# A hybrid attention and RWKV step on one core: the recurrence's products that share a moving operand are joined in pairs

## The chip, the cores and the metric

The kernel runs on one core of a Trainium2 chip (trn2). The metric is the device time of one execution in microseconds. The profile is one execution of the same program, taken by the hardware profiler.

## What is computed

One layer of a streaming encoder, in fp32, for a prompt of 2048 rows and a sample of 32 rows. The projection of the normalised input is split among eight stick-breaking attention heads and eight RWKV-7 heads; both results are joined, projected by `w_out`, and a SwiGLU layer follows. The change touches the RWKV heads, whose definition is a recurrence over the rows:

```python
def _rwkv7_scan(wkv0, r, log_w, k, v, kk, a):
    def step(S, inp):
        r_t, lw_t, k_t, v_t, kk_t, a_t = inp
        sa = jnp.einsum('bhvk,bhk->bhv', S, kk_t)
        S = (S * jnp.exp(lw_t)[:, :, None, :]
             - sa[..., :, None] * (kk_t * a_t)[..., None, :]
             + v_t[..., :, None] * k_t[..., None, :])
        return S, jnp.einsum('bhvk,bhk->bhv', S, r_t)
```

`S` is a state of 64 x 64 for each head. The rows' outputs are then normalised by head, scaled, and written into the mix that the output projection reads.

## The kernel before

The kernel has three stages, one after the other, whose instructions a planner in the build step places on each engine's queue by priority and by when it expects operands and buffers.

The first stage projects the input, and prepares, for each chunk of 64 rows (`CH`; 32 chunks of the prompt and one of the sample) and each head, what the recurrence needs: `QR_d` holds the decayed `kk` and `r` (64 columns each), `KBt_d` the decayed `k` and `kk * a`, `A4_d` their masked products with `QR` (mask `mA`), and `Tinv_d` the inverses of the diagonal blocks of one of them (`inverse`). All are written to DRAM.

The second stage is the one in question. Three generators run in it together: `attention`, `recurrence` and `first_rows` (the output projection of the first 1024 rows). A loop (lines 1170 to 1180) takes the generator that has advanced least, by the work it has yielded (a rough number of microseconds of TensorE) divided by a number of its own: 385 for attention, 230 for the recurrence, which starts at 25, and 155 for the rows, which start at 60. So the yields of the recurrence decide how much of the others' work lies between its steps.

The recurrence works through the chunks in order, the sample first. In each chunk, for eight heads, five groups of small fp32 products go one after the other through one PSUM buffer (`psR`): `up` (line 1095) takes the chunk's `kk` part of `QA` times `VST`, in whose lower partitions are the values and in whose upper ones the state; `sap` (1105) multiplies by the inverse `TTt`; `snp` (1114) multiplies `KBt` by `VS` and gives the new state, which DVE sums (1119) and scales by the decay (1121); `yp` (1127 and 1129) gives the output, `QA`'s `r` part times `VST` plus `AB` times `VS`, which ACT copies into `Yt` (1132). In between, `merge1` and `merge2` complete the inverse of the next chunk by two groups of products of 32 x 32. Each product is issued as two instructions, so a group of eight heads has 16. `fetch` loads the operands of the chunk after the next. After two chunks, `normalise` works on `Yt` on DVE, ACT and POOL in four steps, one at each `step_tail()`, and its columns are transposed and written to the mix.

Attention's products are on operands split into two rounded parts (`fp32r`); its scores become weights by a sigmoid on ACT (777) and a scan along the row on DVE (779), are transposed on TensorE (838), split again by ACT and DVE (105, 106) and multiplied by the values (852, 853).

The third stage finishes the output projection and computes the SwiGLU layer.

Of the kernel before, what the change touches and what calls it, by code (L numbers as in the profile page):

```python
# [24 lines left out]
H = 8  # L25
# [27 lines left out]
def kernel(ctx: ExitStack, tc: tile.TileContext, x_prompt, x_sample, cache_k, cache_v,  # L53
# [61 lines left out]
    with tc.tile_pool(name="pa0", bufs=1) as pe, tc.tile_pool(name="pa1", bufs=1) as pa, \  # L115
# [74 lines left out]
        for r in (0, 64):  # L190
            POOL.affine_select(mA[r:r + 64, 0:64], mA[r:r + 64, 0:64], [[1, 64]], ALU.is_gt, 0.0,
                               base=0, channel_multiplier=-1)
            POOL.affine_select(mA[r:r + 64, 64:128], mA[r:r + 64, 64:128], [[1, 64]], ALU.is_ge, 0.0,
                               base=0, channel_multiplier=-1)
# [69 lines left out]
        def superblock(sb, T0, NTILE):  # L264
# [154 lines left out]
            def g_k(w, c):  # L419
# [47 lines left out]
                def stage3(av, E65, Em, nrm):  # L467
# [6 lines left out]
                    POOL.tensor_tensor(QR[:, 0:NC, 0:64], c3(kk), E65[:, 0:NC, 0:64], ALU.mult)  # L474
                    POOL.tensor_tensor(QR[:, 0:NC, 64:128], c3(rr), E65[:, 0:NC, 1:65], ALU.mult)
# [52 lines left out]
            def inverse(c):  # L528
# [6 lines left out]
                for (jb, nj, d_) in blocks:  # L535
                    for h_ in range(4):
                        SP.dma_start(At[n + h_:n + 4 * nj:4], A4_d[jb:jb + nj, 64 + 32 * d_:96 + 32 * d_, hs + h_,
                                                                   32 * d_:32 * d_ + 32])
# [225 lines left out]
    with tc.tile_pool(reuse_waits="tile", name="bp", bufs=6) as bp, \  # L764
# [237 lines left out]
        def recurrence():  # L1002
# [11 lines left out]
            def fetch(ch):  # L1014
# [5 lines left out]
                KBt = br.tile([P, 512], F32, tag="KBt", name="KBtc")  # L1020
                SP.dma_start(KBt, KBt_d[ch])
                AB = br.tile([P, H, P], F32, tag="AB", name="ABc")
                SP.dma_start(AB[up_], A4_d[ch, 64:128])
# [18 lines left out]
                return [QA, KBt, AB, VS, VST, TTt, T1]  # L1042

            def merge1(c):
# [5 lines left out]
                for h in range(H):  # L1050
                    PE.matmul(mp[96:128, h * 32:(h + 1) * 32], AB[64:96, h, 32:64], T1[64:96, h, :],
# [37 lines left out]
            for ci, ch in enumerate(seq):  # L1089
                samp = ch == NCH  # L1090
                QA, KBt, AB, VS, VST, TTt, _ = cur
                heads = [(h, slice(h * 64, (h + 1) * 64)) for h in range(H)]
                up = psR.tile([P, 512], F32, tag="rw", name="up")
                for h, hs in heads:
                    PE.matmul(up[up_, hs], QA[:, h, 0:64], VST[:, hs], start=True, stop=True)
                Us = br.tile([P, 512], F32, tag="Us", name="Us")
                DVE.tensor_copy(Us[up_], up[up_])
                yield 0.85
# [14 lines left out]
                for h, hs in heads:  # L1113
                    PE.matmul(np_[up_, hs], KBt[:, hs], VS[:, hs], start=True, stop=True)
# [4 lines left out]
                DVE.tensor_tensor(Sn[up_], np_[up_], VST[up_], ALU.add)  # L1119
                s3 = Sn[up_].rearrange("p (h v) -> p h v", h=H)  # L1120
                DVE.tensor_tensor(s3, s3, PC[up_, ch, :].unsqueeze(2).to_broadcast([64, H, 64]), ALU.mult)
                yield 0.85
                step_tail()
                yp = psR.tile([P, 512], F32, tag="rw", name="yp")
                e = 0 if samp else 64 * (ch % 2)
                for h, hs in heads:
                    PE.matmul(yp[e:e + 64, hs], QA[:, h, 64:128], VST[:, hs], start=h == 0, stop=False)
# [344 lines left out]
```

## Time and profile before

| | us |
|---|---|
| median of three runs | 3404.04 |
| lowest and highest run | 3403.97, 3408.7 |
| the profiled execution | 3404.64 |
| its span, first to last instruction | 3402.5 |

In the profile, PE is TensorE's matrix multiplication and PEld its loading of weights, which overlaps it; DVE is VectorE, ACT is ScalarE, POOL is GpSimd and SP is SyncE, which issues DMAs here. A form such as 128*64 128x64 says: 128 rows and 64 columns of weights, and a moving operand of 128 partitions with 64 columns. A row of the timeline merges instructions of one line that follow each other; its duration reaches to the end of the last one, which for PE lies beyond the start of the next row, since products are pipelined. An entry in square brackets is idle time before it and what ended it.

### The profile page before, as it was taken

To read this page: it belongs to the slowest core of one execution; us is meant where nothing else is said; L and a number is where in the kernel's file an instruction comes from. 1 tells how busy PE (TensorE), PEld (TensorE's weight loads), DVE (VectorE), ACT (ScalarE), POOL (GpSimd) and SP (SyncE) were. 2 spreads that over 40 slices of the span, in tenths; PEclk is the share of its full clock that TensorE was granted. 3 is DMA by queue.
4 is the path that set the end of the run, shared out by engine and by line. 5 is a ranking of instruction groups with operands and counts; after the bars stand their busy time and mean duration, and the time that the engine had idled before them with its cause. 6 is when DMAs were issued, how large, how long until landed. Compare 5 with 4: busy or idle time off the path is not lost. (4 is left out here: it accounts for less than half of the span.)

```text
span 3402.5 us, 54147 instructions
## 1 busy us (share of the span) xinstructions
PE 3183.6 (94%) x20661; PEld 2835.4 (83%) x20661; DVE 2233.9 (66%) x3283; ACT 1407.5 (41%) x2768; POOL 1330.4 (39%) x1119
## 2 busy tenths in 40 slices
PE   7998998989779999999998899999899999999998
PEld 7987898878667777877886788899788999899998
DVE  4675757678768887887772566555755555665555
ACT  6434344444245564555542433333422333433333
POOL 3423423244201121112223555555544554466654
PEclk9999999989889999999999999999999999999999
DMA  5555564565675656565544533222633222432221
GB/s 149 157 163 144 165 192 138 154 185 157 198 206 142 165 150 164 150 161 160 156 118 150 183 113 108 83 75 75 206 100 90 84 66 71 144 101 81 81 87 63
DMA packets 542955, 453.74 MB, mean 133 GB/s; under 512 B 74580, under 2 KB 450976, under 8 KB 542696
## 3 DMA queue, kind: packets, MB, share of 16 engines
q1 hardware_dynamic: 454168, 404.26, 41.0%
q10 hardware_dynamic: 88528, 46.02, 5.0%
q8 instruction: 164, 2.69, 0.3%
q14 instruction: 95, 0.78, 0.1%
HBM read 325.64 MB, written 124.53 MB: 132 GB/s over the span
## 5 line engine op out<-in xcount | busy, mean ns | idle before, releaser
L106 POOL TENSOR_TENSOR al<-s,ah 128x512 fp32r<-128x512 f32 x198 | 258.0, 1303 | 558.5 <-ACT ah L105 557.7
L1405 DVE TENSOR_TENSOR x<-x,dn 128x512 f32<-128x512 f32 x374 | 255.1, 686 | 222.8 <-PE dn L1402 222.6
L779 DVE TENSOR_TENSOR_SCAN R<-R,z 128x512 f32<-128x512 f32 (+2 forms) x320 | 338.5, 1084 | 77.2 <-ACT R L777 74.7
L1402 PE MATMUL dn<-dh,hdh 128*128 128x512 f32 x748 | 296.2, 397 | 19.2 <-ACT hdh L105 18.9
L1402 PE MATMUL dn<-dh,hdl 128*128 128x512 f32 x748 | 297.5, 398 | 5.7 <-DVE hdl L106 5.5
L1402 PE MATMUL dn<-dl,hdh 128*128 128x512 f32 x748 | 296.1, 396 | 0.0
L325 PE MATMUL mm<-hh,wh 128*128 128x384 f32 (+4 forms) x1296 | 248.7, 333 | 2.5 <-ACT xp L337 1.5
L105 ACT CAST dh<-rawd 128x1024 fp32r<-128x1024 f32 x66 | 66.2, 1049 | 430.2 <-PE dn L1402 430.2
L105 ACT CAST ah<-s 128x512 fp32r<-128x512 f32 x264 | 163.4, 621 | 183.3 <-PE pt L1356 68.0
L325 PE MATMUL mm<-hh,wl 128*128 128x384 f32 (+4 forms) x1296 | 234.0, 323 | 0.0
L325 PE MATMUL mm<-hl,wh 128*128 128x384 f32 (+4 forms) x1296 | 233.2, 322 | 0.0
L777 ACT ACTIVATE R<-z 128x512 f32<-128x512 f32 (+2 forms) x320 | 163.4, 535 | 159.1 <-PE z L826 98.5
L325 PEld LDWEIGHTS mm<-hh,wh 128*128 128x128 f32 (+1 forms) x1296 | 211.2, 192 | 9.9 <-ACT xp L337 2.2
L325 PEld LDWEIGHTS mm<-hh,wl 128*128 128x128 f32 (+1 forms) x1296 | 210.2, 189 | 2.6
L325 PEld LDWEIGHTS mm<-hl,wh 128*128 128x128 f32 (+1 forms) x1296 | 209.3, 188 | 2.6
L106 DVE TENSOR_TENSOR wtl<-wt,wth 128x512 fp32r<-128x512 f32 (+1 forms) x320 | 179.0, 596 | 15.5 <-ACT wth L105 14.2
L1402 PEld LDWEIGHTS dn<-dh,hdh 128*128 128x128 f32 x748 | 139.2, 186 | 54.6 <-ACT hdh L105 22.3
L105 ACT CAST wth<-wt 128x512 fp32r<-128x512 f32 (+1 forms) x320 | 156.3, 529 | 53.9 <-PE wt L838 51.7
L1402 PEld LDWEIGHTS dn<-dh,hdl 128*128 128x128 f32 x748 | 139.5, 186 | 40.8 <-DVE hdl L106 8.9
L838 PE MATMUL wt<-ident,R 128*128 128x128 f32 x1088 | 164.6, 281 | 9.4 <-DVE wtl L106 8.6
L1029 POOL MEMSET TTt<- 32x512 f32 x33 | 17.2, 521 | 392.5 <-PE sap L1105 272.3
L1402 PEld LDWEIGHTS dn<-dl,hdh 128*128 128x128 f32 x748 | 139.6, 187 | 33.5
(397 smaller groups left out, 7900.6 us busy)
## 6 DMA issues: line engine op xcount, KB each, us to landing
wraw<-in_w_in ACTq DMA_DIRECT2D x77, 512.0 KB
rawu<-in_w_up SPq DMA_DIRECT2D x66, 512.0 KB
rawg<-in_w_gate SPq DMA_DIRECT2D x66, 512.0 KB
rawd<-in_w_down SPq DMA_DIRECT2D x66, 512.0 KB
A_d<-a SPq DMA_DIRECT2D x28, 512.0 KB
mx<-mixT_d SPq DMA_DIRECT2D x27, 512.0 KB
k<-khl_d SPq DMA_DIRECT2D x42, 256.0 KB
vp<-vhl_d SPq DMA_DIRECT2D x42, 256.0 KB
```

The lines of the kernel that those rows point to most:

```text
L105: ACT.copy(hi, src)
L106: (eng or DVE).tensor_tensor(lo, src, f32(hi), ALU.subtract)
L325: PE.matmul(ps[0:wd, 0:s1 - s0], a_[:, kt, 0:wd], b_[:, kt, s0:s1], start=i == 0, stop=i == 3 * KT - 1)
L777: ACT.activation(R[:, 0:n], z[:, 0:n], AF.Sigmoid, scale=-0.125)
L779: DVE.tensor_tensor_scan(rv, rv, z[:, 0:n], before, ALU.mult, ALU.bypass)
L838: PE.transpose(pt[:, j * P:(j + 1) * P], state[h, qg, kc, j][:, kb * P:(kb + 1) * P], ident)
L1029: POOL.memset(TTt[96:128], 0.0)
L1402: PE.matmul(ps[0:n], a_[:, i * P:i * P + n], b_[:, ds_], start=k == 0, stop=k == 3 * len(js) - 1)
L1405: DVE.tensor_tensor(x1[:n, ds_], x1[:n, ds_], ps[0:n], ALU.add)
```

## The change

`up` and `yp`'s first group have the same moving operand, `VST`, and both take half of `QA` as weights: they become one group with 128 output rows, 0 to 63 the first share of the output and 64 to 127 the old `up`. `snp` and `yp`'s second group have the same moving operand `VS` and become one too, with weights `KA`: columns 64 to 127 hold `KBt`, columns 0 to 63 hold `AB`'s output part in the upper partitions and zeros in the lower ones. The two shares of the output can no longer add up in PSUM, since each is in another group: the first is copied with `Us` by DVE, the second by ACT into `y2`, and GpSimd adds them into `Yt`. The halves of `QR` and of the mask change places, so that the rows land on the right partitions. `AB` shrinks to the 32 rows and columns that `merge1` reads, in one buffer. The `yp` step vanishes, and the yields around it with the divisor of the generator (182 for 230) are set anew.

```diff
--- before.py
+++ after.py
@@ -188,9 +188,9 @@
         mA = pe.tile([P, P], F32, name="mA")
         POOL.memset(mA, 1.0)
         for r in (0, 64):
-            POOL.affine_select(mA[r:r + 64, 0:64], mA[r:r + 64, 0:64], [[1, 64]], ALU.is_gt, 0.0,
+            POOL.affine_select(mA[r:r + 64, 64:128], mA[r:r + 64, 64:128], [[1, 64]], ALU.is_gt, 0.0,
                                base=0, channel_multiplier=-1)
-            POOL.affine_select(mA[r:r + 64, 64:128], mA[r:r + 64, 64:128], [[1, 64]], ALU.is_ge, 0.0,
+            POOL.affine_select(mA[r:r + 64, 0:64], mA[r:r + 64, 0:64], [[1, 64]], ALU.is_ge, 0.0,
                                base=0, channel_multiplier=-1)
         DVE.memset(m64, 1.0)
         DVE.memset(m64.rearrange("p (c t) -> p c t", t=CH)[:, :, 0:1], 0.0)
@@ -471,8 +471,8 @@
                                              ALU.mult, ALU.mult)
                     KB = pe.tile([P, 12, P], F32, tag="KB", name="KB")
                     QR = pe.tile([P, 12, P], F32, tag="QR", name="QR")
-                    POOL.tensor_tensor(QR[:, 0:NC, 0:64], c3(kk), E65[:, 0:NC, 0:64], ALU.mult)
-                    POOL.tensor_tensor(QR[:, 0:NC, 64:128], c3(rr), E65[:, 0:NC, 1:65], ALU.mult)
+                    POOL.tensor_tensor(QR[:, 0:NC, 64:128], c3(kk), E65[:, 0:NC, 0:64], ALU.mult)
+                    POOL.tensor_tensor(QR[:, 0:NC, 0:64], c3(rr), E65[:, 0:NC, 1:65], ALU.mult)
                     POOL.tensor_tensor(kk[:, 0:WT], kk[:, 0:WT], av[:, 0:WT], ALU.mult)
                     POOL.tensor_tensor(KB[:, 0:NC, 64:128], c3(kk), c3(Em), ALU.mult)
                     DVE.tensor_scalar(av[:, 0:WT], av[:, 0:WT], -1.0, col(R_KA + c), ALU.add, ALU.mult)
@@ -535,7 +535,7 @@
                 for (jb, nj, d_) in blocks:
                     for h_ in range(4):
                         SP.dma_start(At[n + h_:n + 4 * nj:4], A4_d[jb:jb + nj, 64 + 32 * d_:96 + 32 * d_, hs + h_,
-                                                                   32 * d_:32 * d_ + 32])
+                                                                   64 + 32 * d_:96 + 32 * d_])
                     n += 4 * nj
                 POOL.memset(Ti[0:n], 0.0)
                 POOL.memset(Ti[0:n].rearrange("p a b -> p (a b)")[:, 0:1024:33], 1.0)
@@ -1017,10 +1017,15 @@
                 QA = br.tile([P, H, P], F32, tag="QA", name="QAc")
                 SP.dma_start(QA[up_], QR_d[ch].rearrange("c (e n) t -> n (c e) t", n=64))
                 SP.dma_start(QA[0:64], A4_d[ch, 0:64])
-                KBt = br.tile([P, 512], F32, tag="KBt", name="KBtc")
-                SP.dma_start(KBt, KBt_d[ch])
-                AB = br.tile([P, H, P], F32, tag="AB", name="ABc")
-                SP.dma_start(AB[up_], A4_d[ch, 64:128])
+
+                KA = br.tile([P, H, P], F32, tag="KA", name="KAc")
+                POOL.memset(KA[0:64, :, 0:64], 0.0)
+                SP.dma_start(KA[up_, :, 0:64], A4_d[ch, 64:128, :, 0:64])
+                SP.dma_start(KA[:, :, 64:128], KBt_d[ch].rearrange("p (h n) -> p h n", h=H))
+                AB = None
+                if not samp:
+                    AB = br.tile([P, H, 32], F32, tag="AB", name="ABc", bufs=1)
+                    SP.dma_start(AB[64:96], A4_d[ch, 64:96, :, 96:128])
                 VS = br.tile([P, 512], F32, tag="VS", name="VS")
                 VST = br.tile([P, 512], F32, tag="VST", name="VST")
                 for t in (VST, VS):
@@ -1039,7 +1044,7 @@
                     T1 = br.tile([P, H, 32], F32, tag="T1", name="T1", bufs=1)
                     blocks(TTt[96:128, :, 32:64], 1, 1)
                     blocks(T1[64:96], 0, 0)
-                return [QA, KBt, AB, VS, VST, TTt, T1]
+                return [QA, KA, AB, VS, VST, TTt, T1]
 
             def merge1(c):
                 AB, TTt, T1 = c[2], c[5], c[6]
@@ -1048,7 +1053,7 @@
                 M = br.tile([P, H, 32], F32, tag="M", name="M", bufs=1)
                 mp = psR.tile([P, 512], F32, tag="rw", name="mps")
                 for h in range(H):
-                    PE.matmul(mp[96:128, h * 32:(h + 1) * 32], AB[64:96, h, 32:64], T1[64:96, h, :],
+                    PE.matmul(mp[96:128, h * 32:(h + 1) * 32], AB[64:96, h, :], T1[64:96, h, :],
                               start=True, stop=True)
                 DVE.tensor_copy(M[96:128], mp[96:128, 0:256].rearrange("p (h t) -> p h t", h=H))
                 c[6] = M
@@ -1088,14 +1093,15 @@
             yield 0.85
             for ci, ch in enumerate(seq):
                 samp = ch == NCH
-                QA, KBt, AB, VS, VST, TTt, _ = cur
+                QA, KA, _, VS, VST, TTt, _ = cur
                 heads = [(h, slice(h * 64, (h + 1) * 64)) for h in range(H)]
                 up = psR.tile([P, 512], F32, tag="rw", name="up")
                 for h, hs in heads:
-                    PE.matmul(up[up_, hs], QA[:, h, 0:64], VST[:, hs], start=True, stop=True)
+                    PE.matmul(up[:, hs], QA[:, h, :], VST[:, hs], start=True, stop=True)
+
                 Us = br.tile([P, 512], F32, tag="Us", name="Us")
-                DVE.tensor_copy(Us[up_], up[up_])
-                yield 0.85
+                DVE.tensor_copy(Us, up)
+                yield 0.95
                 if nxt:
                     merge1(nxt)
                 step_tail()
@@ -1111,28 +1117,25 @@
                 yield 0.85
                 np_ = psR.tile([P, 512], F32, tag="rw", name="snp")
                 for h, hs in heads:
-                    PE.matmul(np_[up_, hs], KBt[:, hs], VS[:, hs], start=True, stop=True)
+                    PE.matmul(np_[:, hs], KA[:, h, :], VS[:, hs], start=True, stop=True)
                 if samp or nxt is None:
                     Sn = br.tile([P, 512], F32, tag="STf", name="STf", bufs=1)
                 else:
                     Sn = nxt[4]
                 DVE.tensor_tensor(Sn[up_], np_[up_], VST[up_], ALU.add)
+                e = 0 if samp else 64 * (ch % 2)
+                if e == 0:
+                    Yt = br.tile([P, 512], F32, tag="Yt", name="Yt")
+                y2 = br.tile([64, 512], F32, tag="y2", name="y2")
+                ACT.copy(y2, np_[0:64])
                 s3 = Sn[up_].rearrange("p (h v) -> p h v", h=H)
                 DVE.tensor_tensor(s3, s3, PC[up_, ch, :].unsqueeze(2).to_broadcast([64, H, 64]), ALU.mult)
-                yield 0.85
+                POOL.tensor_tensor(Yt[e:e + 64], Us[0:64], y2, ALU.add)
+                yield 0.95
                 step_tail()
-                yp = psR.tile([P, 512], F32, tag="rw", name="yp")
-                e = 0 if samp else 64 * (ch % 2)
-                for h, hs in heads:
-                    PE.matmul(yp[e:e + 64, hs], QA[:, h, 64:128], VST[:, hs], start=h == 0, stop=False)
-                for h, hs in heads:
-                    PE.matmul(yp[e:e + 64, hs], AB[up_, h, 64:128], VS[up_, hs], start=False, stop=h == H - 1)
-                if e == 0:
-                    Yt = br.tile([P, 512], F32, tag="Yt", name="Yt")
-                ACT.copy(Yt[e:e + 64], yp[e:e + 64])
                 cur = nxt
                 nxt = fetch(seq[ci + 2]) if ci + 2 < len(seq) else None
-                yield 1.7
+                yield 0.1
                 step_tail()
                 if samp:
                     final_state(Sn, sample_wkv)
@@ -1167,7 +1170,7 @@
 
         samp = ExitStack()
         bs = samp.enter_context(tc.tile_pool(name="bs", bufs=2, side="right", reuse_waits="tile"))
-        gens = [[attention(), 0.0, 385.0, 0], [recurrence(), 25.0, 230.0, 0], [first_rows(), 60.0, 155.0, 0]]
+        gens = [[attention(), 0.0, 385.0, 0], [recurrence(), 25.0, 182.0, 0], [first_rows(), 60.0, 155.0, 0]]
         while gens:
             g = min(gens, key=lambda x: x[1] / x[2])
             with priority(tc, g[3]):
```

## Rows read from the trace of the kernel before

**Rows 1.** The page: engine, busy time, share of the span, instructions.
```profile
PE 3183.6 (94%) x20661; PEld 2835.4 (83%) x20661; DVE 2233.9 (66%) x3283; ACT 1407.5 (41%) x2768; POOL 1330.4 (39%) x1119
```

**Rows 2.** Windows: stretch, length, busy of PE, PEld, DVE, ACT, POOL; clock, DMA, GB/s.
```profile
1100.00:1200.00 100.00, 92.05 (x811) 76.33 (x811) 82.94 (x120) 54.59 (x127) 13.26 (x14) 0.95 0.69 174
1200.00:1300.00 100.00, 96.64 (x859) 77.52 (x858) 86.58 (x111) 59.24 (x117) 26.65 (x19) 0.98 0.58 149
...
sum 780.00, PE 753.42 PEld 616.41 DVE 627.99 ACT 410.33 POOL 148.72; mean PE 94.18 PEld 77.05 DVE 78.50 ACT 51.29 POOL 18.59
```

**Rows 3.** The tile of the output projection: count, ns, first and last start.
```profile
L761 PEld LDWEIGHTS mo<-woh,mh x272: 107/188/330, 1271.5 to 1898.4; 128*128 128x128 f32 x128, 128*32 128x32 f32 x8
```

**Rows 4.** Waits, 1040 to 1760 us: who for whom, us in total, times, longest.
```profile
POOL TTt L1029 <- PE sap L1105: 272.3, 22, 23.7
...
ACT R L777 <- PE z L826: 95.4, 74, 5.3
...
PEld wt L838 <- DVE wtl L106: 15.8, 30, 1.3
...
PEld yp L1127 <- DVE VST L1119: 2.5, 8, 0.4
```

**Rows 5.** Timeline of PE, one chunk: start us, us, engine, line, operation, count.
```profile
1208.16 0.48 PE L825 MATMUL z<-k,q 128*128 128x512 f32 x1
...
1209.99 0.39 PE L852 MATMUL av<-wth,vp 128*128 128x512 f32 x1
...
1210.44 0.34 PE L852 MATMUL av<-wth,vp 128*128 128x384 f32 x1
1210.62 0.33 PE L853 MATMUL av<-wtl,vp 128*128 128x384 f32 x1
1210.89 1.15 PE L1127 MATMUL yp<-VST,QAc 128*64 128x64 f32 x16
1211.96 1.14 PE L1129 MATMUL yp<-VS,ABc 64*64 64x64 f32 x16
...
1213.26 0.40 PE L825 MATMUL z<-k,q 128*128 128x512 f32 x1
1213.50 0.40 PE L826 MATMUL z<-k,q 128*128 128x512 f32 x1
...
1215.23 0.40 PE L826 MATMUL z<-k,q 128*128 128x512 f32 x1
1215.46 1.04 PE L838 MATMUL wt<-ident,R 128*128 128x128 f32 x8
```

**Rows 6.** Timeline of PE in an earlier stage: the same columns.
```profile
112.28 1.67 PE L325 MATMUL mm<-hl,wh 128*128 128x416 f32 x8
113.79 1.32 PE L490 MATMUL psb<-bones,rr 128*128 128x2 f32 x12
115.05 0.66 PE L500 MATMUL ptk<-ident,KB 128*128 128x128 f32 x4
```

**Rows 7.** Timeline of DVE in the chunk of rows 5.
```profile
1209.76 0.70 DVE L1119 TENSOR_TENSOR VST<-snp,VST 64x512 f32<-64x512 f32 x1 [0.31 <-PE snp L1114]
1210.49 1.28 DVE L779 TENSOR_TENSOR_SCAN R<-R,z 128x512 f32<-128x512 f32 x1
1211.80 0.69 DVE L1121 TENSOR_TENSOR VST<-VST,PC 64x512 f32<-64x512 f32 x1
```

**Rows 8.** Timeline of POOL, 1549 to 1553 us.
```profile
1549.64 2.40 POOL L748 TENSOR_TENSOR mx<-mx,mh 128x1024 fp32r<-128x1024 f32 x1 [2.72 <-ACT mh L747]
```

**Rows 9.** Line 1087, a memset of 64 x 512: min, median, max ns.
```profile
L1087 POOL MEMSET VST<- x1: 520/520/520, 929.4 to 929.4; 64x512 f32 x1
```

**Rows 10.** DMA queues, 1300 to 1500 us: packets, MB, share of 16 engines.
```profile
q1 hardware_dynamic: 36254, 31.06, 59.7%
```

**Rows 11.** Timeline of SP's DMA issues in the chunk of rows 5.
```profile
1213.88 0.55 SPq L1023 DMA_DIRECT2D ABc<-A_d  x1
```

**Rows 12.** Timeline of DVE beside rows 8.
```profile
1550.18 2.40 DVE L978 SCALAR_TENSOR_TENSOR Yt<-lnst,Yt 128x512 f32<-128x512 f32 x1
```

## The prediction

> **What bounds the kernel now.** I read the page first, for where the time lies, then the table of windows for the stage that the change touches, then single engines inside it. The page shows a PE that is busy nearly everywhere [rows 1]. The table cuts out the stage from 1000 to 1780 us, in which attention, the recurrence and, from 1271.5 us on, the first rows of the output projection share the core [rows 2, 3]. The reader is to see three things there. PE is busy 753 of 780 us, at a granted clock of 0.95 and above in the windows shown. DVE is close behind it in 1100 to 1300 us (83 and 87%) and further away over the whole (628 of 780, 81%). DMA (0.58 to 0.69) and POOL are far from full. The waits of the stage say the same from the other side: ACT waits 95.4 us for PE's scores [rows 4]; POOL's 272 us stand in front of a memset that nobody is late for. So PE's queue, worked off in order, sets the pace, and DVE would be next: PE's own longest wait is for DVE, 15.8 us [rows 4]. The recurrence's chain is not the bound: a chunk's products are spread over some 23 us, 33 times, between attention's.
>
> **What the joined products save on PE.** One chunk has four narrow groups of 16 instructions, `up`, `snp` and two for `yp`, all 64 columns wide. I take their price from the order of PE in one chunk, by what they push apart [rows 5]. An attention product with 512 columns takes 0.23 us from start to start (1209.99, then a second one, to 1210.44). For `up`: from 1213.50 to 1215.23 are 1.73 us, two such products in it are 0.46, which leaves 1.27. For `snp`: 1208.16 to 1209.99 is 1.83, less 0.46 is 1.37. For both groups of `yp`: 1210.62 to 1213.26 is 2.64, less 0.18 for the 384-column product (1210.44 to 1210.62) and 0.12, half of 0.23, for a 256-column one, is 2.34. The sum is 4.98 us a chunk. Where one narrow group follows another it takes 1.07 (1210.89 to 1211.96), so some 0.2 to 0.3 of each price are edges, where neighbours with 128 columns come before and behind.
>
> The joined groups have 128 output rows, so their weights are 128 columns wide. For fp32 data with 64 moving columns this stage has no such row, and I bound the price. The nearest is `psb` of an earlier stage: fp32, 128 x 128 weights, 2 moving columns, 12 products in 115.05 - 113.79 = 1.26 us, 0.105 each; the eight products before it, 416 columns wide, fill 112.28 to 113.79 at 0.19 each, so there is no edge [rows 6]. Eight transposes with 128 columns take 1.04 with the last one's end, at most 0.13 each [rows 5]. A group is then 16 x 0.105 = 1.68 at the lower end; the upper end is two narrow groups, 2.14, with edges. I take 0.11, near `psb`, which has the same weights and type: 1.76 a group, 3.52 for two. Saved are 4.98 - 3.52 = 1.46 us a chunk, **48.2 us** for 33.
>
> **What it adds, and who carries it.** DVE copies `up` from 128 partitions in place of 64, the same 512 elements on each: 0.70, as its other operations of 512 columns out of PSUM [rows 7], and as now. ACT copies the upper half of `np_` in place of `yp`, the same size. GpSimd adds the two shares, 512 columns: half of the 2.40 that it takes for 1024 [rows 8], 1.2 us. The memset for `KA` is 0.52 [rows 9]. Together 1.72 x 33 = 57 us on an engine that is busy 149 of 780 [rows 2]. The add waits for ACT's copy, the memset for `snp`; behind them on POOL are `normalise` and the split of `mx`. POOL already stands for long before the memset of `TTt` without holding anybody; if that cover were gone, the projection's products would wait those 2.40 us for `mx`.
>
> The DMAs: `KBt` goes into `KA` in pieces of 256 B, eight on each partition, half of `AB` likewise, and a third, small load for `merge1` comes. The bytes fall from 512 to 416 KB a chunk, the packets rise by some 1,600. By the mean of the queue, 59.7% of 16 engines over 200 us for 36,254 packets [rows 10], one is 0.053 us, so 1,600 are 84 us of engine time, 5.3 a chunk on each of 16; by bytes it is a small gain. The packets that are added are smaller than the mean, and the loads have most of a chunk to land in, so I take zero. SP gets one issue more, about the 0.55 of `AB`'s now [rows 11]; the `k` and `vp` loads queue behind it, asked for eight steps ahead. The masks, the halves of `QR` and the offset in `inverse` change places, not sizes: nothing.
>
> **What comes back, and what is late next.** First, DVE. In 1100 to 1300 us it is busy 169.5 of 200, with nine chunks; 9 x 1.46 = 13 us less would put it at 91%. There I count half of the gain: twelve chunks lie before the projection starts, so 12 x 0.73 = 8.8 us are lost. Second, `up` of the next chunk follows `snp` after shares of 0.95 + 0.1, where `yp` and 2.55 lay between. With the recurrence's divisor at 182, attention moves on by 1.05 x 385 / 182 = 2.2 us of PE work in that time, the projection by 1.05 x 155 / 182 = 0.9. `up` needs the state summed and scaled on DVE: 0.70 + 0.69 with the starts 0.73 apart, 1.42 us, or 2.73 with a scan of 1.28 between, as in the chunk shown [rows 7]. And the scaling reads two operands from SBUF: such an operation took 2.40 us, where its like takes about 0.7, when POOL's `mx` had begun 0.54 us before it [rows 8, 12]. GpSimd's add can start some 0.6 to 0.7 us after `snp`, the scaling 0.8 at the earliest, so they will meet. I count 0.25 us a chunk, between 0 and 1.9, near the lower end because PE has waited for that sum only 8 times, for 2.5 us in all, though `yp` came right behind it [rows 4]: 8.3 us lost. Third, the recurrence starts at 25/182 of the round in place of 25/230, so attention runs alone for 10.9 units more. A piece of 128 x 512 costs PE 0.46 for scores, 0.52 for four transposes and 0.46 for values, 1.44 [rows 5], and DVE a scan and a split, about 1.28 + 0.70 = 1.98 [rows 7]; 7.6 pieces lose at most 4.1 us, and I count 2. At the end of the stage `yp` leaves the last chain and the add joins it; the projection has products left there [rows 3], so nothing.
>
> The sum: 48.2 - 8.8 - 8.3 - 2 = **29.1 us**. The profiled execution took 3404.64 us, 2.1 more than its span, and stands 0.6 above the median of 3404.04: 3404.64 - 29.1 - 0.6 = 3375 us.
>
> **The rivals.** (a) All of it is gained: PE alone sets the pace. 3404.0 - 48.2 = 3356, with `psb`'s price 3351. For it: ACT's waits for PE; against it: DVE's 87%. (b) The edges belong to fp32 groups among neighbours of the rounded type, and not to narrow ones. Then each joined group has them too: 1.76 + 0.3 = 2.06, saved 4.98 - 4.12 = 0.86 x 33 = 28.4, given back 5.2 + 8.3 + 2: 3391. Against it stands `psb`, fp32 and without edges [rows 6]. (c) A joined group costs just what two narrow ones cost, edges and all: 2 x 1.27 to 2 x 1.37 for `up` with its share of `yp` and the same for `snp`, against 4.98: saved at most 0.2 us a chunk, 7 us, and given back as much: 3404. The Trainium skill has a rule that points there: TensorE: Matmul & The Clock Gate, LDWEIGHTS (loading the stationary operand), says that a load's time goes with its columns, 107 ns for 128 and 53 for 64; by it two narrow groups (2 x 16 x 53 ns = 1.71 us) equal one joined group (16 x 107 ns), an estimate, and only edges are left to gain. The trace is a little kinder, 2.14 for two against 1.68 to 1.76. (d) **Slower**: the chain from `snp` to `up` comes to the front. If GpSimd's add wins the race each time and a scan lies between, the chain is 2.73 + 1.2 = 3.9 us against 2.2 of cover before the projection's pieces come; a wait of 1.7 x 33 = 56 us eats the 48: 3412. It decides from a wait of 1.46 us a chunk. For it: a scan does lie between sum and scaling in the chunk shown. Against it: four attention products in between hide 0.9 of it. That the change does nothing is excluded by its form: 16 fewer matmul calls in a chunk.
>
> **How the numbers follow.** My forecast 0.56, (a) 0.14, (b) 0.12, (c) 0.09, (d) 0.09. A difference within 0.2%, 6.8 us, is about what can't be told from no change. Faster: my forecast, (a) and most of (b), 0.80; same: most of (c) and the edges of (b) and (d), 0.11; slower: most of (d), 0.09. The range goes from the cheapest joined group with everything gained, 3350, to (b) and the better part of (c), 3403; left out are (d) and a part of (c).
>
> **What would show it.** Right: `up` and `snp` as 128*128 groups of 16 with 0.10 to 0.12 from start to start and no gap around them, 3.5 us a chunk; the stage 29 us shorter, DVE at 85% or more in 1100 to 1300; the other stages unmoved. Wrong: gaps around the joined groups (b), 0.14 a product (c), PE waiting before `up` for the scaling by more than 0.5 us a chunk, or scalings of 1.5 to 2 us (d); also loads of `KA` that land so late that `snp` waits.

## The result and the profile after

The changed kernel took 3496.8 us (median of four runs, 3488.19 to 3509.44) beside 3404.35 us for the kernel before: a ratio of 1.027, interval 1.0254 to 1.0285. It is 92 us slower, where 29 us less was forecast. Its profiled execution took 3488.19 us.

The page of the kernel after, busy time of each engine, with its share of the span and its instructions:

```profile
PE 3221.4 (92%) x19605; PEld 2862.5 (82%) x19605; DVE 2243.0 (64%) x3283; ACT 1412.3 (41%) x2768; POOL 1392.2 (40%) x1185
```

PE has 1056 instructions less than before [rows 1] and is busy 38 us longer. Where that lies, the views of single tiles tell (durations in ns, then first and last start): the first scores `z` mark the start of the stage in question, the last values `av` its end. The first two lines are those of before, the others those of after:

```profile
L825 PEld LDWEIGHTS z<-k,q x320: 186/188/337, 945.4 to 1757.6; 128*128 128x128 f32 x160
...
L853 PE MATMUL av<-wtl,vp x320: 272/393/776, 959.6 to 1776.5; 128*128 128x512 f32 x128, 128*128 128x256 f32 x32
...
L825 PEld LDWEIGHTS z<-k,q x320: 186/188/337, 945.7 to 1837.6; 128*128 128x128 f32 x160
...
L853 PE MATMUL av<-wtl,vp x320: 272/393/795, 959.8 to 1861.7; 128*128 128x512 f32 x128, 128*128 128x256 f32 x32
...
L761 PEld LDWEIGHTS mo<-woh,mh x272: 106/188/337, 1273.8 to 1985.9; 128*128 128x128 f32 x128, 128*32 128x32 f32 x8
```

The stage begins at the same time and ends 85 us later (831 us become 916); the projection starts as before [rows 3]. All that is lost is lost here: the profiled executions differ by 84 us. The windows of after (columns as in rows 2):

```profile
1100.00:1200.00 100.00, 91.37 (x727) 74.85 (x726) 87.98 (x123) 57.99 (x131) 20.83 (x23) 0.97 0.57 145
1200.00:1300.00 100.00, 90.70 (x578) 72.84 (x578) 74.98 (x94) 48.15 (x94) 27.83 (x23) 0.86 0.50 123
1300.00:1400.00 100.00, 93.94 (x623) 76.91 (x622) 67.44 (x86) 42.89 (x85) 24.47 (x22) 0.88 0.54 133
...
1500.00:1600.00 100.00, 89.97 (x554) 72.06 (x554) 68.87 (x86) 43.53 (x86) 27.58 (x23) 0.86 0.49 123
```

Against rows 2 the engines do less in 1200 to 1300 us: DVE 75 for 87, ACT 48 for 59, DMA 0.50 for 0.58, PE 91 for 97, at a granted clock of 0.86 for 0.98; only POOL, far from full, does 1 us more. So no engine has become the bound; PE stands more, and it spends time at 1.2 GHz instead of 2.4. By the clock's records that is 143 us of 1000 to 1870 us, for 34 us before. The waits of the stage (1040 to 1850 us; us in total, times, longest) say for whom:

```profile
ACT wth L105 <- PE wt L838: 117.9, 87, 8.1
POOL KAc L1022 <- PE snp L1120: 114.8, 30, 7.6
...
DVE wtl L106 <- ACT wth L105: 56.1, 52, 4.5
...
PEld wt L838 <- DVE wtl L106: 40.3, 67, 2.3
PEld z L825 <- DVE R L779: 37.3, 57, 2.3
```

The same waits in before, beside rows 4 (1040 to 1760 us):

```profile
ACT wth L105 <- PE wt L838: 41.9, 52, 2.6
...
PEld z L825 <- DVE R L779: 11.2, 21, 1.0
...
DVE wtl L106 <- ACT wth L105: 9.1, 10, 2.3
```

PE waits 40.3 us before `wt` where it waited 15.8 [rows 4], and 37.3 for 11.2 for the scan before `z`; ACT and DVE stand in the same circle, ACT 117.9 us for 41.9 before the transposes, DVE 56.1 behind ACT for 9.1. These are attention's products, which the change does not touch. How they come to wait, PE's order shows (the columns of rows 5; in brackets idle time and what ended it):

```profile
1410.65 0.39 PE L852 MATMUL av<-wth,vp 128*128 128x512 f32 x1
1410.96 0.66 PE L838 MATMUL wt<-ident,R 128*128 128x128 f32 x4
1411.37 0.48 PE L853 MATMUL av<-wtl,vp 128*128 128x512 f32 x1
1411.69 0.49 PE L838 MATMUL wt<-ident,R 128*128 128x128 f32 x3
1411.93 0.48 PE L852 MATMUL av<-wth,vp 128*128 128x512 f32 x1
1412.25 0.40 PE L853 MATMUL av<-wtl,vp 128*128 128x512 f32 x1
1414.49 0.79 PE L838 MATMUL wt<-ident,R 128*128 128x128 f32 x3 [1.85 <-DVE wtl L106]
...
1418.40 1.97 PE L1111 MATMUL sap<-Us,TTt 64*64 64x64 f32 x16
...
1424.20 3.51 PE L1120 MATMUL snp<-VS,KAc 128*128 128x64 f32 x16
...
1431.68 2.12 PE L761 MATMUL mo<-woh,mh 128*128 128x512 f32 x8
1433.63 1.90 PE L1100 MATMUL up<-VST,QAc 128*128 128x64 f32 x16
1435.34 2.10 PE L761 MATMUL mo<-wol,mh 128*128 128x512 f32 x8
...
1437.91 2.07 PE L761 MATMUL mo<-woh,mx 128*128 128x512 f32 x8
```

The transposes of attention come close behind each other, cut into pieces of four and three, and then PE stands for the buffer (`psW` has two) that ACT and DVE have to empty first. After that the clock is at its lower level, 0.53 granted over 14 us (the window below, columns as in rows 2): `sap` takes 1.97 us where it took 1.14 in before (second line below), and the joined `snp` 3.51 us.

```profile
1415.00:1429.00 14.00, 14.00 (x85) 11.98 (x86) 4.80 (x8) 3.63 (x8) 2.31 (x3) 0.53 0.34 71
...
1434.36 1.14 PE L1105 MATMUL sap<-Us,TTt 64*64 64x64 f32 x16
```

The three groups of a projection block (`mo`) come within 6 us around `up`; in before they lie further apart. The order of a queue is laid in the build, so the trace shows a plan that has become worse, and the question for the experiments was what made it so.

### The profile page after: what moved, and what is told of

Same layout as the page of the kernel before. It is cut to its first block, busy times and chain, and to the rows that moved or that the text cites. A ratio compares the mean times of both kernels' runs of the same rounds, so it can differ in the third digit from the quotient of the medians.

```text
span 3486.2 us, 52185 instructions
## 1 busy us (share of the span) xinstructions
PE 3221.4 (92%) x19605; PEld 2862.5 (82%) x19605; DVE 2243.0 (64%) x3283; ACT 1412.3 (41%) x2768; POOL 1392.2 (40%) x1185
## 3 DMA queue, kind: packets, MB, share of 16 engines
q1 hardware_dynamic: 507224, 400.98, 40.3%
## 5 line engine op out<-in xcount | busy, mean ns | idle before, releaser
L838 PE MATMUL wt<-ident,R 128*128 128x128 f32 x1088 | 186.8, 295 | 33.3 <-DVE wtl L106 31.6
L838 PEld LDWEIGHTS wt<-ident,R 128*128 128x128 f32 x1088 | 132.7, 149 | 74.6 <-DVE wtl L106 47.0
L825 PE MATMUL z<-k,q 128*128 128x512 f32 (+2 forms) x320 | 141.0, 441 | 42.9 <-DMA k<-khl_d 21.9
L1405 PEld LDWEIGHTS dn<-dh,hdl 128*128 128x128 f32 x748 | 139.0, 186 | 40.3 <-DVE hdl L106 8.5
```

The costliest lines, as they stand in the source:

```text
L825: PE.matmul(z[:, 0:n], state[h, qg][:, 0, js], k[:, 0:n], start=True, stop=False)
L838: PE.transpose(pt[:, j * P:(j + 1) * P], state[h, qg, kc, j][:, kb * P:(kb + 1) * P], ident)
L1405: PE.matmul(ps[0:n], a_[:, i * P:i * P + n], b_[:, ds_], start=k == 0, stop=k == 3 * len(js) - 1)
```

## The experiments

In the table, "stage" runs from the first `z` to the end of the last `av`. "Close pairs" counts, from 1050 us on, the tiles `wt` (270 to 290) between whose last transpose and the first of the second tile behind it, the next user of its buffer, PE has less than 2.6 us of products, each at its full-clock rate; both are worked out from PE's records. The counts depend on the rates taken: with rates some per cent off, single counts move by up to 15. "Low" is the time at the lower clock in 1000 to 1870 us. The last three columns are of the profiled execution, which can lie up to 15 us from the median (e14); most kernels ran two or three times.

| kernel | us | ratio (95%) | stage | close pairs | low |
|---|---|---|---|---|---|
| before | 3404 | | 831 | 62 | 34 |
| after | 3497 | 1.0254 to 1.0285 | 916 | 124 | 143 |
| e1 | 3495 | 1.022 to 1.032 | 932 | 137 | 184 |
| e2 | 3408 | 0.998 to 1.002 | 837 | 59 | 31 |
| e3 | 3473 | 1.017 to 1.023 | 900 | 117 | 126 |
| e4 | 3428 | 1.004 to 1.010 | 848 | 50 | 48 |
| e5 | 3469 | 1.014 to 1.024 | 904 | 128 | 100 |
| e6 | 3466 | 1.015 to 1.021 | 896 | 77 | 68 |
| e7 | 3403 | 0.997 to 1.001 | 826 | 51 | 65 |
| e8 | 3493 | 1.023 to 1.029 | 914 | not counted | 140 |
| e9 | 3482 | 1.019 to 1.028 | 902 | 139 | 139 |
| e10 | 3473 | 1.016 to 1.025 | 898 | 135 | 126 |
| e11 | 3456 | 1.011 to 1.020 | 883 | 95 | 72 |
| e12 | 3467 | 1.014 to 1.023 | 893 | 134 | 102 |
| e13 | 3487 | 1.020 to 1.027 | 911 | 128 | 123 |
| e14 | 3494 | 1.015 to 1.036 | 933 | 135 | 170 |
| e15 | 3488 | 1.020 to 1.027 | 914 | 108 | 126 |
| e16 | 3427 | 1.003 to 1.009 | 852 | 81 | 51 |
| e17 | 3381 | 0.989 to 0.995 | 803 | 48 | 34 |
| e18 | 3405 | 0.998 to 1.001 | 798 | 55 | 48 |

**Spacing (e1, e2).** After with the yields and the divisor of before, and before with those of after:

```diff
...
-        gens = [[attention(), 0.0, 385.0, 0], [recurrence(), 25.0, 182.0, 0], [first_rows(), 60.0, 155.0, 0]]
+        gens = [[attention(), 0.0, 385.0, 0], [recurrence(), 25.0, 230.0, 0], [first_rows(), 60.0, 155.0, 0]]
```

> The changed kernel with the yields of the kernel before (0.85, and 1.7 where yp stood) and its divisor 230: joined products and GpSimd's add as changed, only the spacing of the recurrence among attention is the old one. Theory P (the new spacing puts the steps of the chain so near each other that PE stands and loses its clock): back to 3360 to 3400 us. Theory G (ACT's copy waits for DVE's sum, GpSimd's add then blocks DVE's scaling): 3470 to 3500, as changed. Theory W (joined groups cost PE more than the rows of before let expect, and the clock falls with them): 3470 to 3500 too.

> The kernel before with the yields of the changed one (0.95, 0.95, 0.1 and the divisor 182), its four narrow groups kept. Theory P: 3450 to 3500 us. Theories G and W: 3395 to 3415, no difference.

Neither moves: the numbers of the loop are not the cause.

**Width (e4, e5).** Before with `up` alone widened to 128 columns, its lower half unused; and after with each joined group issued as two narrow ones (the same for `np_`):

```diff
-                    PE.matmul(up[:, hs], QA[:, h, :], VST[:, hs], start=True, stop=True)
+                    PE.matmul(up[up_, hs], QA[:, h, 64:128], VST[:, hs], start=True, stop=True)
+                for h, hs in heads:
+                    PE.matmul(up[0:64, hs], QA[:, h, 0:64], VST[:, hs], start=True, stop=True)
```

> The kernel before with up alone widened to 128 weight columns (the lower half of its result is not used) and the halves of QA swapped for it; yp stays as it is, spacing as before. PE's work grows by 16 x (0.11 - 0.06) = 0.8 less the edges of 0.3, so 0.5 us a chunk, 16 us. Theory W: 3440 us or more, with the clock below 1 far more often. Theories P and G: 3404 to 3425, the clock as before.

> The changed kernel with each joined group issued as two narrow ones of 64 columns into the same tile; copies, GpSimd's add, the missing yp step and the spacing as changed. Theory W (the wide groups themselves: their loads leave TensorE half empty, PE falls behind and its clock falls with it): 3400 to 3435 us, the clock at 0.96 or more. Theory S (the structure: with yp gone, up stands right behind snp and its two evacuations, PE waits there, and the waits take the clock down): 3470 to 3510, the clock as changed, 0.95 or less.

e4 prices a wide group: from its first product to what follows, `up` takes 58.9 us in 33 chunks for 36.3, 22.6 more, of which some 4 come back on the product in front of it (below, at the terms of the sum); the stage takes 16 us more and the run 23. e5 keeps most of the loss without any wide group, so the width does not carry it.

**The evacuation and the chain (e3, e8, e9, e10).** DVE adds both shares straight from PSUM; ACT's copy of the second share stands ahead of DVE's sum (3493 us, 1.0259); the state's way back is cut; the second share is left out:

```diff
-                ACT.copy(y2, np_[0:64])
-                POOL.tensor_tensor(Yt[e:e + 64], Us[0:64], y2, ALU.add)
+                DVE.tensor_tensor(Yt[e:e + 64], np_[0:64], Us[0:64], ALU.add)
...
-                    Sn = nxt[4]
+                    Sn = br.tile([P, 512], F32, tag="STf", name="STj", bufs=1)
```

> The changed kernel with the two shares added by DVE straight out of PSUM; ACT's copy y2 and GpSimd's add are gone, DVE gets 0.69 us a chunk more. Theory G: 3375 to 3410 us, and the scaling takes 0.69 in every chunk again. Theories P and W: 3480 to 3520.

> The changed kernel with ACT's copy of the output share issued ahead of DVE's sum on the same PSUM tile, not behind it. Theory G (ACT's queue stands because of DVE's): 3465 to 3475 us. Theories W and S: 3480 to 3500, the sum only waits for the copy in its turn.

> The kernel after, with the state's way back cut: the new state is still computed and written, to a tile that nobody reads, and the state half of VST is zeroed by a GpSimd memset each chunk instead. So the recurrence leaves out the states of earlier chunks (they are not in the result), while nearly every product, sum and copy is still issued. What goes is the chain from snp over the sum and the scaling to the next up. Theory (TensorE stands before up and before attention's products because this chain ends late, and then runs at the lower clock): most of the 92 us go, 3395 to 3425, with the time at the lower clock in the recurrence's stage back from 143 us to under 60. Rival (the loss is in evacuating the joined tiles, not in the state's chain): 3470 to 3495. Rival (fewer columns on TensorE lower its clock whatever it waits for): above 3450 with over 100 us at the lower clock, but no waits before up.

> The kernel after, with the second share of the output left out of the result: ScalarE's copy of it and GpSimd's sum of the two shares are gone, GpSimd copies the first share alone. Theory (state chain and the order of TensorE's queue): the time falls by about what adding on VectorE gave, 15 to 35 us, to 3455 to 3475, and the waits before wt stay. Rival (the evacuation of the shares by ScalarE and GpSimd is the loss): 3400 to 3425.

e9 overthrew the theory I had by then: without the chain from `snp` to `up` most of the loss stays (3482 us). Without GpSimd's sum 24 us come back in e3, and as much in e10, which leaves out the copy too. e3 lies between what its theories gave.

**More work on PE (e6, e7, e11), a second buffer (e12).** After with the old groups of `yp` still issued and unused; before with `up` and `yp`'s first group joined alone, so that `yp`'s second group stays as a step of its own; after with a useless product ahead of `up`; after with two PSUM buffers for the recurrence:

```diff
+                PE.matmul(up, ident, QA[:, 0:4, :], start=True, stop=True)
```

> The joined groups as changed, and the two old groups of yp issued behind snp as well, in their old place and with the old spacing; only 8 columns of their result are copied by ACT and nothing uses them. PE gets 70 us of work that is not needed. Theory S: the work fills PE's waits between snp and up: 3400 to 3480 us, the clock at 0.96 or more. Theory W: PE pays it on top, 3540 us or more.

> Only up and yp's first group are joined; snp stays narrow, yp's second group stays behind it, ACT copies it and GpSimd adds; spacing as before. By prices: up wider +22 us (as e4_wide_up measured), one narrow group of yp less, -35: 3390 us. Theory S: 3385 to 3410, since PE has work between snp and up. Theory W: half of the change's loss, 3430 to 3450.

> The kernel after, with one product that nobody needs (float32, 512 columns, into up's tile, overwritten by the true group) ahead of every up: by the time of such columns about 0.86 us a chunk, 28 us of TensorE in all. Theory (TensorE stands before up and loses its clock): the product lies in time in which TensorE stood, and it keeps the clock: 3465 to 3495, not slower than the kernel after, with fewer us at the lower clock. Rival (TensorE's own work is the bound, waits are scattered): 28 us more, 3510 to 3525.

> The kernel after, with two PSUM buffers for the recurrence's tile instead of one (the projection's tile takes its turn in the same two). Theory 1 (up waits for the scaled state, not for the buffer that sum and copy have to empty): within 10 us of the kernel after, 3478 to 3498. Theory 2 (the single buffer holds up back behind the sum and ScalarE's copy): a third or more of the 92 us come back, 3400 to 3460.

e6 and e11 give PE more to do and end 30 and 41 us sooner than after; so PE's work is not what after pays for. In both the close pairs and the time at the lower clock fall. e12's second buffer gives 30 us back, between its two theories. e7 joins one pair and loses nothing. It lacks what every kernel has that is over 1% slower: the tile `KA`.

**The tile KA (e13, e14, e15, e16).** Its zeros set once in two lasting tiles; three buffers for `KA`, `VS` and `VST`; the projection's block loaded one block ahead; and e7 with `KA`'s memset and the load of `KBt` into it, but without the joined `snp`:

```diff
-                KBt = br.tile([P, 512], F32, tag="KBt", name="KBtc")
-                SP.dma_start(KBt, KBt_d[ch])
+                KBt = br.tile([P, H, P], F32, tag="KA", name="KAc")
+                POOL.memset(KBt[0:64, :, 0:64], 0.0)
+                SP.dma_start(KBt[:, :, 64:128], KBt_d[ch].rearrange("p (h n) -> p h n", h=H))
```

> The kernel after, but the zeros of KA are set once, in two tiles that live through the recurrence, in place of a GpSimd memset in each chunk that waits for snp (114.8 us of waiting in the profile after). Theory M (that memset holds up the split of mx that stands behind it on GpSimd's queue, so the projection's products come late and in a bunch): a good part of the 92 us comes back, 3400 to 3450, and the projection's three groups of a block spread again over more than 10 us. Rivals (the loads' waits, or the number of steps): 3475 to 3500.

> The kernel after, with three buffers in place of two for KA, VS and VST, so that a chunk's memset and loads no longer wait for the snp just issued. Theory L (SyncE's queue stands before the load of KA until snp, 13.6 us at 1414 to 1428 us, with all other loads behind it, so that the projection's operands come late and its products in a bunch): 3400 to 3450. Theory M gives the same here, as the memset no longer waits either. Rival (neither; the bunching comes from the missing step behind snp): 3475 to 3500.

> The kernel after, with the load of the projection's next block (mx) asked for one block ahead. Theory (the projection's three groups come in a bunch because their operand lands late, and the bunch leaves attention alone in the rest of the chunk): the groups of a block spread again, first to third above 10 us in place of 6, and 20 to 80 us come back, 3410 to 3470. Rival (the bunch has another cause): 3480 to 3500 and unchanged spreads.

> The kernel of the run e7 (only up and the first group of yp joined, 0.999 of before), with KA's layout in place of KBt's: a GpSimd memset of the lower left quarter in each chunk and the load of KBt in pieces of 256 bytes; the products are those of e7. Theories M and the small pieces of the loads: 3440 to 3490. Rival (the memset and the small pieces cost nothing, as the prediction took it): 3395 to 3412.

The memset that waits 114.8 us is not the cause: without it e13 is 10 us faster, and the intervals overlap. Nor are the loads' waits for `snp`, though e14's two runs lie 30 us apart (3479 and 3509). e15 is a lesson on symptoms: the projection's groups lie apart again (first to third 17 us on average over the first eight blocks, for 6 in after and 15 in before), attention's close pairs fall only to 108, and the time by 9 us. e16 has the product list of e7 and costs 23 us more, between the ranges of its theories. With the memset acquitted by e13, the pieces of the load are left: `KBt` goes into `KA` in runs of 64 columns, 256 bytes.

**The pieces alone (e17), and the true data in whole rows (e18).** First e17's lines for those of after, then e18's one load in their place, of a `KA_d` that the first stage writes:

```diff
-                POOL.memset(KA[0:64, :, 0:64], 0.0)
-                SP.dma_start(KA[up_, :, 0:64], A4_d[ch, 64:128, :, 0:64])
-                SP.dma_start(KA[:, :, 64:128], KBt_d[ch].rearrange("p (h n) -> p h n", h=H))
+                SP.dma_start(KA[up_, 4:8].rearrange("p h n -> p (h n)"), Z_d[ch % 2, 64:128])
+                SP.dma_start(KA[:, 0:4].rearrange("p h n -> p (h n)"), Z_d[ch % 2])
...
+                SP.dma_start(KA, KA_d[ch])
```

> The kernel after, but KA lives in two tiles zeroed once, and its two loads bring zeros from DRAM in pieces of 2 KB instead of the data in pieces of 256 bytes; bytes, waits and products stay. So snp and the second share of the output are left out of the result. Theory P (the 256-byte pieces of KA's loads change the order in which attention's work is laid on the queues, worth 23 us in e16 with two thirds of the pieces): 3430 to 3465, with half or more of the low-clock time gone. If the pieces are the whole cause: 3385 to 3415. Rival (the missing step behind snp is the cause and the pieces cost nothing here): 3475 to 3495.

> The kernel after with the whole computation, and KA laid out in the first stage: there the transposed KBt is copied into columns 64 to 127 of a tile whose columns 0 to 63 take the output part of AB (a GpSimd copy of 64 partitions) and zeros, and this tile goes to DRAM; a chunk's KA then comes in one load of whole rows of 4 KB, 512 KB, and needs no memset. Theory P (the 256-byte pieces are the whole cause): the stage of the recurrence as in e17, with its last product for the values at about 1745 us, plus what the copies (two of 64 x 256 for each four chunks and two heads) and 8.6 MB more to write cost the first stage, 0 to 20 us: 3378 to 3405. Rival (e17 was fast because its data were zeros or its loads had no producer): 3460 to 3500.

e17, with the joined products and the sums of after, is 27 us faster than before and 116 faster than after. The kernel that is nearest to it is e13, which has no memset in the chunks either: against it the loads alone changed (long pieces, of zeros, from a tensor that is written once), and it is 106 us faster. No theory had it so fast. PE's order in it, at the place shown for after:

```profile
1420.01 0.34 PE L853 MATMUL av<-wth,vp 128*128 128x384 f32 x1
1420.18 0.34 PE L854 MATMUL av<-wtl,vp 128*128 128x384 f32 x1
1420.36 1.89 PE L1128 MATMUL snp<-VS,KAc 128*128 128x64 f32 x16
1422.06 0.47 PE L826 MATMUL z<-k,q 128*128 128x512 f32 x1
1422.38 0.39 PE L827 MATMUL z<-k,q 128*128 128x512 f32 x1
1422.61 0.40 PE L826 MATMUL z<-k,q 128*128 128x512 f32 x1
...
1423.08 1.03 PE L839 MATMUL wt<-ident,R 128*128 128x128 f32 x8
...
1424.36 1.94 PE L1108 MATMUL up<-VST,QAc 128*128 128x64 f32 x16
1426.11 0.47 PE L826 MATMUL z<-k,q 128*128 128x512 f32 x1
...
1427.12 1.04 PE L839 MATMUL wt<-ident,R 128*128 128x128 f32 x8
1427.91 2.10 PE L762 MATMUL mo<-woh,mx 128*128 128x512 f32 x8
```

Scores, transposes and values come in whole sets of two again, with a group of the recurrence or the projection between the sets. e18 shows that neither the zeros nor the missing producer of e17 is the reason: with all data, in one load of whole rows, its stage, from 980.2 to 1778 us, is shorter still. Its first and last rows:

```profile
L832 PEld LDWEIGHTS z<-k,q x320: 186/188/337, 980.2 to 1759.8; 128*128 128x128 f32 x160
...
L860 PE MATMUL av<-wtl,vp x320: 272/393/793, 994.3 to 1777.4; 128*128 128x512 f32 x128, 128*128 128x256 f32 x32
```

What the stage gains (831 to 798, 34 us) the first stage loses, since `KA` is put together there: it ends at 980.2 for 945.4 us, 35 us later, more than the 20 us that I had allowed. The sum is 0.9996 of before, no change.

## Why the prediction was wrong

**The step that failed** is the paragraph on the DMAs, "I take zero". It had the right object, `KBt` "in pieces of 256 B, eight on each partition", counted 1,600 more packets and 84 us of DMA engine time a chunk, and then set the cost to nothing because the loads had most of a chunk to land in. e17 measures it: 106 us for the pieces of both loads of `KA` (against e13), 116 with the memset (against after). No rival held it, so the range could not.

The pieces do not cost that much by themselves. Where a step with `yp` still stands behind `snp`, they cost little: 23 us in e16 (`KBt`'s load and a memset), and by estimate 10 to 20 in e6, which has both loads and is 60 us above before, some 40 to 50 of them for its added products. As far as these runs show, it is the short pieces together with the vanished step that cost over 100.

**Not by the way I had looked for.** I had asked whether the loads land late or fill the queue. The queues of after from 1300 to 1500 us (columns of rows 10), under the count of packets by size, and above both the count of before:

```profile
DMA packets 36275, 31.35 MB, mean 157 GB/s; under 512 B 9204, under 2 KB 27124, under 8 KB 36254
...
DMA packets 43185, 26.22 MB, mean 131 GB/s; under 512 B 20402, under 2 KB 36818, under 8 KB 43169
...
q1 hardware_dynamic: 43169, 26.01, 52.6%
```

Packets under 512 bytes are 20,402 for 9,204 before, but the engines are busy 52.6% of the time for 59.7% [rows 10], and PE's waits for a DMA in 1040 to 1850 us are 3 us in all. The Trainium skill, DMA: Bandwidth & Descriptors, Specifications, names 512 bytes as the least transfer that runs at line rate. The trace of after agrees: in these 200 us its packets of 256 bytes moved 12.3 KB per us of their time, those of 512 bytes 15.5 and those of 2 KB 18.2. But a packet of 256 bytes took only 21 ns, where I had reckoned with 53, and over all packets the rate while busy falls only from 31.06 MB in 1910 us of engine time (16.3 KB per us) to 26.01 MB in 1683 (15.5). So the loss is not on the DMA engines. It is in the queues of the others: the planner lays the instructions by when it expects operands, and with these loads it lays another order on PE, ACT and DVE. That the order goes with the pieces is shown: the sequence of the 640 scans and splits of attention on DVE is one and the same in after and e13, and one and the same in e17 and e18; between the two pairs 92 places differ, between e17 and before 10. Other changes move the order too: e6 and e16, with short pieces but a `yp` step, come within 24 and 30 places of e17, and there the pieces cost little. That it differs because the planner reckons long landing times for short pieces is argued from how it works; no run shows its reckoning. No run has the short pieces in just e17's order, so that the loss goes through the order alone is argued as well, from waits that are for DVE and ACT and not for loads. Nor does a run tell how much of it each part of the order carries.

**From the order to the time.** The worse order shows in the close pairs, 124 for 62, and costs twice: PE stands before `wt`, `z` and `up`, and it does more of its work at 1.2 GHz, where a joined group takes 3.51 us for 1.89. Adding up what the products of the stage took beyond their full-clock rates from start to start, from 1000 us on: the lower clock costs 67.5 us in after for 12.7 before, and waits of over 0.25 us each 98.5 for 34.8, together 118 us more; less the 31 us that the groups save from first product to follower (below) that is 87, and the stage grew by 85. In e17 the same working gives some 8 and 48.

**The terms of the sum.** With the pieces gone, in e17, the rest of the sum comes out nearly as forecast. From first product to follower all four narrow groups take 145.0 us in before, 4.39 a chunk, a group 1.07 (median). But they also leave edges on their neighbours, as the chunk of rows 5 shows:

```profile
1213.26 0.40 PE L825 MATMUL z<-k,q 128*128 128x512 f32 x1
1213.50 0.40 PE L826 MATMUL z<-k,q 128*128 128x512 f32 x1
1213.82 1.15 PE L1095 MATMUL up<-VST,QAc 128*64 128x64 f32 x16
1214.90 0.50 PE L825 MATMUL z<-k,q 128*128 128x512 f32 x1
1215.23 0.40 PE L826 MATMUL z<-k,q 128*128 128x512 f32 x1
1215.46 1.04 PE L838 MATMUL wt<-ident,R 128*128 128x128 f32 x8
```

An attention product of 512 columns takes 0.23 us among its like, 0.32 right before `up` and 0.33 right behind it. Over the stage these edges come to 21 us in before, so that the groups cost 5.0 a chunk, near the 4.98 of the forecast. The two joined groups take 114.4 us in e17, 3.47 a chunk, near the 3.52 of the forecast and near `psb` [rows 6]; they have next to no edge in front (1420.18 to 1420.36 above, 0.18 for 384 columns) and one behind (1422.06 to 1422.38, 0.32), some 7 us in all, which the forecast left out. So about 45 us are saved for the 48.2. Of these e17's stage keeps 28, so some 17 are given back, for the 19.1 of the forecast. Waits of over 0.25 us come to 13 us more there than in before, 8 more before `up` and 7 before `wt`, less a little elsewhere, which is the size of what I had counted for the chain and for DVE (87% busy in 1200 to 1300 us). That the causes are those I named is not shown: the profile puts only 0.9 us before `up` down to the scaled state, and most of the rest to ACT. (ACT copies the lower half of `np_`, where the prediction says the upper; the size is the same.)

**The rivals.** (b) is half right: joined groups do have an edge, but only behind. (c), a joined group at the price of two narrow ones, falls with 114.4 against 145.0; its own figures, four times 1.27 at the least, already come to 5.08 against 4.98 and leave nothing to save. (d), the chain to `up`, came first to mind, as PE does wait some 18 us before `up` in after; e9 cuts the chain and keeps most of the loss. That DVE's scaling meets GpSimd's add was seen (1.4 to 2.7 us in 12 of 33 chunks, for 0.69 in rows 7), and without that add (e3) 24 us come back; but in e17 they meet as well (1.1 to 1.9 us in 10 chunks). "Also loads of `KA` that land so late that `snp` waits" stood last among the signs to look for, with no price: the loads were the cause, but `snp` never waited for one.

## What to carry to other kernels

When tiles are merged to merge products, look at what the merge does to the runs of bytes in the loads, and price that by a kernel that changes the loads alone, in the schedule in which they will stand; laying the merged tile out where it is produced keeps the runs long, but then that stage pays. Where a planner orders the queues, a change that adds no engine's work can go with a much worse order: compare the order of untouched work, here attention's transposes, before looking at the changed instructions. A stall that one finds beside the change (the memset's 114.8 us, the bunched projection, the chain) is a cause only when its removal moves the time. And a group of small products costs what it adds to its neighbours too: 21 us of 166 here.

## What the runs showed of the hardware

A float32 product with 128 x 128 weights and 64 moving columns costs 0.107 us from start to start in a row of 16 (1.71 us a group) at the full clock, and a group takes 3.27 us at the lower (seven of the ten that ran there in after); with 64 columns of weights a group takes 1.07, so a joined group costs 1.6 narrow ones. In before a narrow group makes the 512-column products in front of it and behind it some 0.1 us longer each; in e17 a joined group does so only behind it. More work on PE can shorten a run: e6 adds some 70 us of products to after (66 narrow groups) and e11 some 28, and both end 30 to 41 us sooner, with 68 and 72 us at the lower clock for 143. DMA queues with over twice as many packets under 512 bytes moved 15.5 KB per us of busy time for 16.3.
